# A mixed mLSTM and gMLP encoder on one core: three heads' ways down by Strassen's seven products, and values tile by tile

## The chip, the cores and the metric

One core of a Trainium2 chip runs the whole program. The metric is the device time of one execution in microseconds (us), the median of several runs. The engines are TensorE (PE in the profile; its weight loads are PEld), VectorE (DVE), ScalarE (ACT), GpSimd (POOL) and SyncE (SP), which here only issues DMAs.

## The reference, cut to what matters

The input has 512 tokens of 1024 numbers. Two layers each run a SwiGLU feed-forward network (FFN), a mixer, a second FFN and a gated embedding, each followed by a residual and a layer norm. The mixer of layer 0 is the mLSTM, and the change is in it alone:

```
def mlstm_mixer(x, w_in, b_in, conv_w, norm_g, w_out):
    proj = x @ w_in + b_in                                   # 1024 -> q, k, v, z, gates
    qk, v, z, gates = jnp.split(proj, [...], axis=-1)
    qk = jax.nn.silu(causal_depthwise_conv(qk, conv_w))      # 4 taps
...
    h = mlstm_cell(q, k, v, ig, fg)                          # 4 heads, q and k 256 wide, v 512 wide
    h = ((h - mu) * lax.rsqrt(var + LN_EPS)).reshape(B, S, ML_INNER) * norm_g
    h = (h * jax.nn.sigmoid(z)).astype(x.dtype)
    return h @ w_out                                         # 2048 -> 1024: the way down
```

A head's way down is a product of its 512 x 512 piece of h (tokens by features) with its 512 x 1024 piece of w_out, and the four heads' products are added up.

## The kernel before, in words

**Precision.** Every large product is made from two halves of each operand: a high half (whi, xh, hh) rounded to fp32r and a low half (wlo, xl, hl) with the rest. `mm3` issues three matmuls for one: high by high, low by high, high by low (lines 263 to 265). A matmul of 128 rows by 512 columns is the unit that this document counts.

**Weights.** The class `Weights` holds one list of weight tiles for the whole program, in the order in which TensorE takes them. SyncE loads a raw tile (wraw; three buffers); `fill` splits it into a free pair of whi and wlo, four of which are in the pool "main" and two in "extra" during the mLSTM. ACT makes whi (L188). VectorE makes wlo by a subtraction (L194), or, where the caller says `low="dma"`, ACT writes the negated low half and GpSimd's queue adds the raw tile to it by an accumulating DMA (L191, L192). `take` hands the next pair to the code that issues matmuls; `release` frees it and splits the next tile in the list, so the split's instructions stand in the engines' queues at the place of the release.

**mLSTM, one head after another** (`mlstm`, heads h = 0 to 3):

- `project_qk` makes four tiles, q0, q1, k0, k1, each of 24 matmuls (tile qps). VectorE then does the convolution (pad, one acc and three more, L933 to L938), ACT the silu, and ACT and VectorE the split (qh, ql, L268 and L269).
- `project_v` makes v token block by token block: for each of four blocks 24 matmuls over the four quarters of the weights (vps), then VectorE adds the bias (vf, L969), and a split follows (vh, vl).
- `scores` makes S for the four blocks j (sps, 24 matmuls); ACT makes the decay (ex), VectorE multiplies (sf, L1010) and a split follows (sh, sl). The banks alternate between the two sets of four PSUM banks, "up" and "dn".
- `project_z` makes z0 and z1 (zps, 24 matmuls each); ACT takes the sigmoid (sz) and VectorE multiplies by the norm's gain (L981).
- `mix` makes h for t = 3, 2, 1, 0 (nps, 60 matmuls in all). VectorE and, for one small power, GpSimd normalise each t in a chain of some eleven instructions (L1037 to L1049, ending in hn).
- z2 and z3 follow; then the way down of the head before (`down`, tile dps, 96 matmuls): for each token block four tiles of weights by two halves of the columns, and VectorE adds the two banks to the residual xt (L565, L563).
- `gate_turn` transposes hn (hps, 16 small matmuls, L1064), VectorE multiplies by sz (hzf, L1067), and a split gives hh and hl. In the last head the four transposes stand between the token blocks of the way down of head 2, and the last head's own way down with the norm follows.

**Strassen in the FFNs.** The class `Group` makes a product of 512 tokens, 512 features and 1024 columns from seven half-size products instead of eight. A product is twelve matmuls (gps). `Weights.forms` lists the seven weight tiles for it: b11, b21, t2 = (b22 − b12) + b11, t1, b12, b22, b21, of which t2 and t1 are each made by two VectorE instructions in place on the raw tiles (L104 and L105, L109 and L110). `form` makes the left operand of a product (fhi, flo; for some of them sums of half size first, L725 to L730), `product` issues the matmuls, `add` adds the two banks to the residual. Products 0, 1 and 3 start a pair of banks; product 2 accumulates on top of product 0, 4, 5 and 6 on top of what is there. The mLSTM doesn't use it before.

Of the kernel before, what the change touches and what calls it, by code (L numbers as in the profile page):

```python
# [16 lines left out]
P = 128  # L17
# [29 lines left out]
class Weights:  # L47
# [4 lines left out]
    def __init__(self, nc, raw_pool, split_pool):  # L52
        self.nc = nc
        self.pools, self.free = {"main": split_pool}, {"main": W_BUFS, "none": 0}
        self.raw_pools, self.raw_bufs = {"raw": raw_pool}, {"raw": RAW_BUFS}
        self.loads, self.left, self.raws = [], [], {}
        self.queues, self.held_raws = defaultdict(deque), defaultdict(deque)
        self.order, self.next_split = [], 0
# [32 lines left out]
    def forms(self, quarter, kind, raw_kind):  # L91

        vec = self.nc.vector
        b11, b12, b22, b21 = (self.add_load(quarter(i, j), n, raw_kind)
                              for i, j, n in ((0, 0, 2), (0, 1, 1), (1, 1, 1), (1, 0, 2)))
        raw = self.raws

        def as_loaded(j):  # L100
            return lambda: (raw[j], (j,))

        def t2():
            vec.tensor_sub(raw[b12], raw[b22], raw[b12])  # L104
            vec.tensor_add(raw[b11], raw[b12], raw[b11])  # L105
            return raw[b11], ()

        def t1():
            vec.tensor_sub(raw[b21], raw[b21], raw[b11])  # L109
            vec.tensor_sub(raw[b11], raw[b22], raw[b11])  # L110
            return raw[b11], (b11,)

        return [(kind, (b11,), as_loaded(b11)), (kind, (b12, b22, b21), as_loaded(b21)), (kind, (), t2),
                (kind, (), t1), (kind, (), as_loaded(b12)), (kind, (), as_loaded(b22)), (kind, (), as_loaded(b21))]
# [22 lines left out]
    def load(self, only=None, between=None):  # L137


        for kind, queue in self.queues.items():  # L140
            held = self.held_raws[kind]
            while held and not self.left[held[0]]:
                held.popleft()
            if queue and len(held) < self.raw_bufs.get(kind, 0) and only in (None, kind):
# [4 lines left out]
                size = 2048 if kind == "raw" else 1024  # L149
                name = "wraw" if kind == "raw" else "wquarter"  # L150
                raw = self.raw_pools[kind].tile([P, size], F32, name=name, tag=name)
# [13 lines left out]
    def fill(self, most=1000, low=None):  # L165
        while most and self.next_split < len(self.order):
# [19 lines left out]
            for i in range(parts):  # L186
                s = slice(i * shape[1] // parts, (i + 1) * shape[1] // parts)
                self.nc.scalar.activation(hi[:, s], src[:, s], AF.Copy)  # L188
                if low == "dma":
# [3 lines left out]
                else:  # L193
                    (low or self.nc.vector).tensor_sub(lo[:, s], src[:, s], hi[:, s].bitcast(F32))  # L194
# [38 lines left out]
def hybrid_trunk(ctx: ExitStack, tc, x, p, ln_g, ln_b, ffn1_wgu, ffn1_wd, ffn2_wgu, ffn2_wd,  # L233
# [21 lines left out]
    ps_dn = ctx.enter_context(tc.tile_pool(name="ps_dn", bufs=4, space=PSUM))  # L255
# [18 lines left out]
    def dn_bank(name):  # L274
        return ps_dn.tile([P, 512], F32, name=name, tag="dn")
# [78 lines left out]
    def ml_weights():  # L354
# [3 lines left out]
        def o_w(h):  # L358
            add_rows(wout, 4 * h, 4)

        for h in range(HEADS):
# [6 lines left out]
            if h:  # L368
                o_w(h - 1)
# [1032 lines left out]
```

## Time and profile before

| | |
|---|---|
| median of 3 runs | 2247.41 us (2246.97 to 2248.39) |
| the profiled execution's time, its span | 2248.24 us, 2246.5 us |
| mean granted TensorE clock | 0.999 |
| TensorE busy | 2234.0 us, 99% |
| VectorE busy | 1439.3 us, 64% |
| ACT busy | 886.3 us, 39% |
| matmuls recorded | 10649 |
| first q projection of heads 0, 1, 2, 3 | at 387, 451.7, 552.2 and 652.8 us |
| end of the mLSTM's last way down | at 778 us |

A row of the timeline is start, duration, engine, line, operation, output <- inputs, shape, count; in brackets the idle time before it and what ended that. A row of the grouped view is line, engine, operation, output <- inputs, shape, count | busy us, mean ns | idle before and what ended it. Matmuls overlap, so the time of a run of them is read from start to start.

### The profile page before, as it was taken

Reading aid. Unit: us, or ns where it says so; the run is one execution under the profiler, and the core shown is the slowest. Engines: PE = TensorE matmul, PEld = TensorE weight load, DVE = VectorE, ACT = ScalarE, POOL = GpSimd, SP = SyncE. Lnnn points to the kernel's source line nnn. Section 1 sums busy time; section 2 is a strip of 40 time slices with the busy share of each in tenths; the row PEclk is TensorE's granted clock in tenths of the full one; section 3 lists DMA queues with packets and bytes.
Section 4 is the critical chain, followed back from the end, with each engine's and each line's share of the span. In section 5 each row is a group of like instructions: output and inputs, shape, how many; then the busy total and the mean of one; then the engine's idle time right before and its main releaser. Section 6 shows DMA issues by size and latency. Waiting matters only on the chain.

```text
span 2246.5 us, 26356 instructions
## 1 busy us (share of the span) xinstructions
PE 2234.0 (99%) x10649; PEld 1875.2 (83%) x10649; DVE 1439.3 (64%) x2083; ACT 886.3 (39%) x1241; POOL 103.2 (5%) x136
## 2 busy tenths in 40 slices
PE   9999999999999999999999999999999999999998
PEld 8888888888888888888889888888888888888887
DVE  5566667765555656666687566666756566666677
ACT  3333336454544433333344333335344452333332
POOL 1000000111121000000000000000010100000000
PEclk9999999999999999999999999999999999999999
DMA  7322223376674534331333332222356453432221
GB/s 237 114 94 93 94 85 100 81 177 123 150 152 106 155 113 131 104 103 57 112 122 122 111 95 95 94 85 94 122 141 141 104 167 98 130 113 85 84 85 57
DMA packets 200754, 254.08 MB, mean 113 GB/s; under 512 B 5636, under 2 KB 155268, under 8 KB 200632
## 3 DMA queue, kind: packets, MB, share of 16 engines
q1 hardware_dynamic: 166864, 211.83, 29.1%
q0 software_dynamic: 27152, 25.87, 7.8%
q10 hardware_dynamic: 6616, 14.69, 2.0%
q8 instruction: 84, 1.38, 0.2%
q14 instruction: 38, 0.31, 0.0%
HBM read 224.58 MB, written 2.11 MB: 101 GB/s over the span
## 4 chain that ended last, share of the span: by engine, by line
PE 97%; DMA 1%; ACT 1%; issue 1%; DVE 0%; SPq 0%; POOL 0%; DVEq 0%; POOLq 0%
PE fps L265 13%; PE fps L263 13%; PE fps L264 13%; PE gps L265 6%; PE gps L263 6%; PE gps L264 6%; PE dps L264 5%; PE dps L265 5%; PE dps L263 5%; PE gups L263 1%; PE zps L263 1%; PE gvps L265 1%; PE zps L265 1%; PE gups L264 1%; PE gups L265 1%; PE zps L264 1%
## 5 line engine op out<-in xcount | busy, mean ns | idle before, releaser
L263 PE MATMUL fps<-xh,whi 128*128 128x512 f32 x1312 | 510.7, 389 | 0.0
L264 PE MATMUL fps<-xl,whi 128*128 128x512 f32 x1312 | 510.5, 389 | 0.0
L265 PE MATMUL fps<-xh,wlo 128*128 128x512 f32 x1312 | 510.4, 389 | 0.0
L194 DVE TENSOR_TENSOR wlo<-wraw,whi 128x1024 fp32r<-128x1024 f32 (+1 forms) x284 | 341.7, 1217 | 183.3 <-ACT whi L188 182.2
L188 ACT ACTIVATE whi<-wraw 128x1024 fp32r<-128x1024 f32 (+1 forms) x333 | 344.2, 1048 | 219.3 <-PE fps L264 103.2
L264 PEld LDWEIGHTS fps<-xl,whi 128*128 128x128 f32 x1312 | 246.3, 188 | 51.2
L265 PEld LDWEIGHTS fps<-xh,wlo 128*128 128x128 f32 x1312 | 246.3, 188 | 51.1
L263 PEld LDWEIGHTS fps<-xh,whi 128*128 128x128 f32 x1312 | 246.3, 188 | 50.9
L194 DVE TENSOR_TENSOR wlo<-wquarter,whi 128x1024 fp32r<-128x1024 f32 x112 | 137.2, 1225 | 202.1 <-ACT whi L188 202.1
L188 ACT ACTIVATE whi<-wquarter 128x1024 fp32r<-128x1024 f32 x112 | 118.7, 1060 | 237.8 <-PE gps L265 177.8
L265 PE MATMUL gps<-whi,flo 128*128 128x512 f32 x448 | 174.3, 389 | 0.0
L264 PE MATMUL gps<-wlo,fhi 128*128 128x512 f32 x448 | 174.3, 389 | 0.0
L263 PE MATMUL gps<-whi,fhi 128*128 128x512 f32 x448 | 174.3, 389 | 0.0
L790 ACT ACTIVATE sg<-fps 128x512 f32<-128x512 f32 x80 | 47.9, 598 | 280.8 <-PE fps L265 280.8
L565 DVE TENSOR_TENSOR xt<-xt,gps 128x512 f32<-128x512 f32 x224 | 143.0, 679 | 0.0
L268 ACT ACTIVATE fhi<-h 128x512 fp32r<-128x512 f32 x112 | 69.4, 625 | 115.9 <-DVE h L726 45.8
L263 PE MATMUL dps<-whi,hh 128*128 128x512 f32 x256 | 101.5, 396 | 0.0
L264 PE MATMUL dps<-wlo,hh 128*128 128x512 f32 x256 | 100.5, 393 | 0.0
L265 PE MATMUL dps<-whi,hl 128*128 128x512 f32 x256 | 100.3, 392 | 0.0
L269 DVE TENSOR_TENSOR flo<-h,fhi 128x512 fp32r<-128x512 f32 x112 | 75.6, 687 | 36.4 <-ACT fhi L268 36.4
L264 PEld LDWEIGHTS gps<-wlo,fhi 128*128 128x128 f32 x448 | 84.1, 188 | 17.5
L263 PEld LDWEIGHTS gps<-whi,fhi 128*128 128x128 f32 x448 | 84.1, 188 | 17.4
(277 smaller groups left out, 3852.4 us busy)
## 6 DMA issues: line engine op xcount, KB each, us to landing
wraw<-in_ffn_wgu_dram SPq DMA_DIRECT2D x79, 1024.0 KB, 5.4
wquarter<-in_ffn_wd_dram SPq DMA_DIRECT2D x64, 512.0 KB, 3.8
wlo<-wraw POOLq DMA_DIRECT2D x49, 512.0 KB, 7.6
wraw<-in_ml_w_in_dram SPq DMA_DIRECT2D x24, 1024.0 KB, 5.7
wraw<-in_gm_w_in_dram SPq DMA_DIRECT2D x15, 1024.0 KB, 5.6
wraw<-in_ffn_wd_dram SPq DMA_DIRECT2D x12, 1024.0 KB, 5.0
wraw<-in_ffn_wgu_dram SPq DMA_DIRECT2D x17, 512.0 KB, 3.9
wraw<-in_ml_w_out_dram SPq DMA_DIRECT2D x8, 1024.0 KB, 5.3
```

Source lines behind the costliest of these rows:

```text
L188: self.nc.scalar.activation(hi[:, s], src[:, s], AF.Copy)
L194: (low or self.nc.vector).tensor_sub(lo[:, s], src[:, s], hi[:, s].bitcast(F32))
L263: mm(ps, st[0], mv[0], start=start, stop=False, skip_group_check=more)
L264: mm(ps, st[0], mv[1], start=False, stop=False, skip_group_check=more)
L265: mm(ps, st[1], mv[0], start=False, stop=stop, skip_group_check=more)
L268: sca.activation(hi, src, AF.Copy)
L269: vec.tensor_sub(lo, src, hi.bitcast(F32))
L565: vec.tensor_add(dst, dst, ps)
L790: sca.activation(sg, ps, AF.Silu)
```

## The change

**The ways down of heads 0, 1 and 2 go by `Group`**, and their products are spread over the head that follows. A function `step` does, in this order: add the product before to the residual, issue the next product, release its weight pair (which splits the next tile of the list), and make the form for the product after the next. Heads 1 to 3 call it after q1 (product 0), k0 (product 1), k1 (product 2), after v's quarters 0, 1 and 3 (products 3, 4, 5), and after z3 (product 6; in the last head between the second and third transposes). The addition of product 5 stands after the scores, that of product 6 right behind product 6. `ML_SLOTS` puts the seven weight forms at these places in the list of weights. They come from two raw loads per head: one sits in one of the three raw buffers for three uses, the other in the tile that holds the norm's two vectors (now one tile, "gb", loaded just before the last way down). Raw buffers are therefore freed out of order (`raw_free`). Forms made in place never get their low half by DMA.

**v of heads 1 to 3** goes over weight quarters outside and token blocks inside: four up banks are open at once, so the four vf, vh and vl all come in the last quarter. Head 0 stays as it was.

**Around them:** all scores of heads 1 to 3 use the up banks; z2 moves into the mixing, between t = 1 and t = 0; t = 1 of the mixing and the transposes of odd t use dn banks, which are handed out by number, and those that hold a group's sums are pinned; hf of heads 0 to 2 is kept whole, without a split after the transposes; fewer weight tiles are released with `low="dma"` (16 in place of 34). The last head's own way down stays a plain one of 96 matmuls.

```diff
-    def forms(self, quarter, kind, raw_kind):
+    def forms(self, kind, b11, b12, b22, b21):
...
-                if low == "dma":
+                if low == "dma" and make not in self.in_place:
...
+    ML_SLOTS = (1, 2, 3, 4, 5, 7, 11)
...
             if h:
-                o_w(h - 1)
-        o_w(HEADS - 1)
+                tiles = W.order[at:]
+                del W.order[at:]
+                k = 4 * h - 4
+                j0, j1 = W.add_load(kp(wout)[:, k:k + 2, :], 3), W.add_load(kp(wout)[:, k + 2:k + 4, :], 3, "gb")
+                left, right = ((slice(None), slice(None), slice(c, c + 512)) for c in (0, 512))
+                down_w = W.forms("", (j0, left), (j0, right), (j1, right), (j1, left))
+                for i, tile_i in enumerate(tiles):
+                    W.order.append(tile_i)
+                    if i in ML_SLOTS:
+                        W.order.append(down_w[ML_SLOTS.index(i)])
+        add_rows(wout, 4 * HEADS - 4, 4)
...
         def add(self):
+
             r = self.next_add
+            if r == self.next_product:
+                return
             self.next_add += 1
             i, j = self.TO[r]
             for e, ps in enumerate(self.banks[r % 2]):
-                residual(2 * i + e, j, ps, False)
+                residual(2 * i + e, j, ps, r in self.first)
+                if r >= 5:
+                    del pinned[id(ps)]
...
                     W.release(low="dma")
+                    if i:
+                        step()
...
+                banks = [up_bank("vps") for _ in range(TB)]
+                for k in range(4):
+                    w = W.take()
+                    for t, ps in enumerate(banks):
+                        for kb in (2 * k, 2 * k + 1):
+                            mm3(ps, xs(kb, t * P, (t + 1) * P), [a[:, kb % 2] for a in w], kb == 0, kb == KB - 1)
+                        if k == 3:
+                            take(t, ps)
+                    W.release(low="dma" if k < 2 else None)
+                    if k != 2:
+                        step()
                 return vh, vl
...
-                W.release(later=i < 2, low="dma")
-                run_affine()
+                W.release(later=h == 0 or i > 0)
+                if h == 0:
+                    run_affine()
...
-                    ps = (dn_bank if j % 2 else up_bank)("sps")
+                    ps = (dn_bank if j % 2 and h == 0 else up_bank)("sps")
...
-                    bank = up_bank if t >= 2 else dn_bank
+                    if t == 0:
+                        between()
+                    bank = dn_bank if t == 1 else up_bank
...
+            def step(later=False):
+
+                if group is not None:
+                    group.add()
+                    group.product()
+                    W.release(later=later)
+                    group.form()
...
-                hn = mix(h, ss, v)
-                W.refill(4)
-                for i in range(2, 4):
-                    project_z(h, sz, i)
...
-                if prev is not None:
-                    down(prev, h == 1, low=[None, None, "dma", "dma"] if last else ["dma"] * 4,
-                         between=turn if last else None)
-                else:
-                    norm = Norm(0, 1)
-                if not last:
+                hn = mix(h, ss, v, lambda: project_z(h, sz, 2))
...
+                project_z(h, sz, 3)
+                if h < HEADS - 1:
+                    step(True)
+                    if group is not None:
+                        group.add()
                     hs, turn = gate_turn(h, hn, sz)
                     for t in range(TB):
                         turn(t)
-                prev = hs
-            down(prev, False, norm)
+                    group = Group(hs, fpool, h == 0)
+                    group.form()
+                    group.form()
+                    W.refill(4)
+            hs, turn = gate_turn(h, hn, sz)
+            for t in range(TB):
+                turn(t)
+                if t == 1:
+                    step(True)
+                    group.add()
+            W.refill(4)
+            norm = Norm(0, 1)
+            down(hs, False, norm)
```

The changed kernel's line numbers are higher than those of the profile before, by 13 in `mm3` and `split` and by up to 65 in the mLSTM. Three places in the order of VectorE's instructions follow, each before and after the change.

**VectorE while head 1's q and k are projected.** acc and pad belong to the convolution, ql is the low half of q or k. Before:

```order
L938 SCALAR_TENSOR_TENSOR acc<-pad,cols,acc 128x512 x3
L269 TENSOR_TENSOR ql<-acc,qh 128x512
L933 MEMSET pad 128x3
L936 TENSOR_SCALAR acc<-pad,cols 128x512
L938 SCALAR_TENSOR_TENSOR acc<-pad,cols,acc 128x512 x3
L269 TENSOR_TENSOR ql<-acc,qh 128x512
```

After, the same stretch from q1's convolution to the first addition of the group (wraw<-wraw are the two weight sums of t1, hf<-hf the sums of the left operand, flo its low half, xt<-xt,gps the addition of product 0):

```order
L282 TENSOR_TENSOR ql<-acc,qh 128x512
L110 TENSOR_TENSOR wraw<-wraw 128x2x512
L111 TENSOR_TENSOR wraw<-wraw 128x2x512
L207 TENSOR_TENSOR wlo<-wraw,whi 128x1024
L756 TENSOR_TENSOR hf<-hf 128x2x256
L757 TENSOR_TENSOR hf<-hf 128x2x256
L282 TENSOR_TENSOR flo<-hf,fhi 128x512
L972 MEMSET pad 128x3
L975 TENSOR_SCALAR acc<-pad,cols 128x512
L977 SCALAR_TENSOR_TENSOR acc<-pad,cols,acc 128x512 x3
L282 TENSOR_TENSOR ql<-acc,qh 128x512
L594 SCALAR_TENSOR_TENSOR xt<-xt,gps 128x512 x2
```

Six instructions of the group have come between two convolutions that stood next to each other, and the addition stands behind the second.

**VectorE from the values to the scores of head 1.** vf, vl belong to v, sf and sl to the scores. Before:

```order
L269 TENSOR_TENSOR vl<-vf,vh 128x256 x2
L969 TENSOR_TENSOR vf<-vps,vb 128x512
L269 TENSOR_TENSOR vl<-vf,vh 128x256 x2
L194 TENSOR_TENSOR wlo<-wraw,whi 128x1024
L1010 SCALAR_TENSOR_TENSOR sf<-sps,ex 128x512
```

After:

```order
L1009 TENSOR_TENSOR vf<-vps,vb 128x512
L282 TENSOR_TENSOR vl<-vf,vh 128x256 x2
L207 TENSOR_TENSOR wlo<-wraw,whi 128x1024
L596 TENSOR_TENSOR xt<-xt,gps 128x512 x2
L207 TENSOR_TENSOR wlo<-wraw,whi 128x1024
L1070 SCALAR_TENSOR_TENSOR sf<-sps,ex 128x512
```

An addition (of product 4) and a second low half stand ahead of the first sf. The four rounds of vf and vl in front of these rows are as many as before; they were one per 24 matmuls of vps, and now all four belong to the last 24.

**VectorE at the end of the last head.** hzf and hl follow the transposes, dps is a plain way down. Before:

```order
L1067 TENSOR_TENSOR hzf<-hps,sz 128x512
L269 TENSOR_TENSOR hl<-hzf,hh 128x4x128
L194 TENSOR_TENSOR wlo<-wraw,whi 128x1024 x2
L565 TENSOR_TENSOR xt<-xt,dps 128x512 x2
L1067 TENSOR_TENSOR hzf<-hps,sz 128x512
L269 TENSOR_TENSOR hl<-hzf,hh 128x4x128
L565 TENSOR_TENSOR xt<-xt,dps 128x512
```

After, from the end of the normalising on:

```order
L207 TENSOR_TENSOR wlo<-wraw,whi 128x1024 x3
L1040 TENSOR_SCALAR sz<-sz,cols 128x512
L1132 TENSOR_TENSOR hzf<-hps,sz 128x512
L282 TENSOR_TENSOR hl<-hzf,hh 128x4x128
L1132 TENSOR_TENSOR hzf<-hps,sz 128x512
L282 TENSOR_TENSOR hl<-hzf,hh 128x4x128
L596 TENSOR_TENSOR xt<-xt,gps 128x512 x2
```

The transposes' work, which was spread between the blocks of the way down of head 2, now stands close together behind three low halves, and the addition of product 6 behind its first half.

165 lines of the change are left out of this document (98 added, 67 removed).

## The prediction

> **What bounds the kernel now.** First the page, its busy times and its chain of waits:
>
> ```profile
> PE 2234.0 (99%) x10649; PEld 1875.2 (83%) x10649; DVE 1439.3 (64%) x2083; ACT 886.3 (39%) x1241; POOL 103.2 (5%) x136
> PE 97%; DMA 1%; ACT 1%; issue 1%; DVE 0%; SPq 0%; POOL 0%; DVEq 0%; POOLq 0%
> ```
>
> TensorE is busy for 99% of the span and is 97% of the chain that ended last. A matmul taken away there is time taken away, as long as nothing makes TensorE wait. Second, the windows view of one head of the mLSTM, all engines (each cell is busy us and a count; then granted clock, DMA share, GB/s):
>
> ```profile
> 450.00:551.00 101.00, 101.00 (x489) 85.00 (x488) 57.63 (x120) 48.40 (x71) 14.60 (x17) 1.00 0.62 149
> ```
>
> In these 101 us TensorE has no gap at all, at full clock, and VectorE (third cell) works for 57%. A mean hides where VectorE's work is bunched, and the change puts its new work on VectorE at fixed places. So the question is whether VectorE's answers still come before TensorE asks for them.
>
> **Part 1, what goes: 36 matmuls in each of three heads.** The windows view of tile dps on TensorE for the ways down after heads 1, 2 and 3, then TensorE's timeline at the first one's two ends, and at one Strassen product in a feed-forward stage:
>
> ```profile
> 527.00:552.00 25.00, 22.56 (x96) 1.00 0.79 172
> 627.00:653.00 26.00, 22.57 (x96) 1.00 0.78 168
> 729.00:753.80 24.80, 23.31 (x96) 1.00 0.48 126
> ```
>
> ```profile
> 528.17 0.40 PE L263 MATMUL dps<-whi,hh 128*128 128x512 f32 x1
> ...
> 550.57 0.38 PE L1064 MATMUL hps<-ident,hn 128*128 128x128 f32 x2
> ...
> 862.75 0.39 PE L263 MATMUL gps<-whi,fhi 128*128 128x512 f32 x1
> ...
> 865.47 0.39 PE L263 MATMUL fps<-xh,whi 128*128 128x512 f32 x1
> ```
>
> The first way down takes 550.57 − 528.17 = 22.40 us. The second has the same busy time and gets the same 22.40. The third is broken up by transposes and 0.75 busier; part of that is records overlapping at the breaks, so I take 22.7 (22.4 to 23.15). Together 67.5. A product of twelve matmuls takes 2.72, and 21 of them 57.1. That saves 10.4. If the products ran at the pace of the ways down, 22.40/96 = 0.233 each, they would cost 58.8 and save 8.7.
>
> Fewer weight tiles get their low half by a DMA, which removes a wait that the grouped view shows today:
>
> ```profile
> L264 PE MATMUL vps<-wlo,xh 128*128 128x512 f32 x128 | 49.9, 390 | 0.2 <-DMA wlo<-wraw 0.2
> L264 PEld LDWEIGHTS vps<-wlo,xh 128*128 128x128 f32 x128 | 24.0, 188 | 5.5 <-DMA wlo<-wraw 0.7
> ```
>
> [...]
>
> **Part 2, what comes: VectorE's chain before product 2.** Product 2 accumulates into the banks that product 0 used, so it waits for VectorE to have added product 0 to the residual. That addition stands behind the convolutions of q and k, two pairs of weight sums, the splits and a pair of half sums. VectorE takes all that in order; nothing can overtake. Its timeline in head 0 (the convolution), then in a feed-forward stage (the Strassen work), and the page's row for the high half of a weight tile:
>
> ```profile
> 462.39 0.49 DVE L936 TENSOR_SCALAR acc<-pad,cols 128x512 f32<-128x512 f32 x1 [0.25 <-ACT pad L934]
> ...
> 465.19 0.06 DVE L933 MEMSET pad<- 128x3 f32 x1
> ...
> 469.47 0.68 DVE L269 TENSOR_TENSOR ql<-acc,qh 128x512 fp32r<-128x512 f32 x1
> ...
> 862.47 1.22 DVE L109 TENSOR_TENSOR wquarter<-wquarter 128x1024 f32<-128x1024 f32 x1
> 863.72 1.22 DVE L110 TENSOR_TENSOR wquarter<-wquarter 128x1024 f32<-128x1024 f32 x1
> ...
> 866.81 1.22 DVE L194 TENSOR_TENSOR wlo<-wquarter,whi 128x1024 fp32r<-128x1024 f32 x1 [1.86 <-ACT whi L188]
> 867.95 1.22 DVE L194 TENSOR_TENSOR wlo<-wraw,whi 128x1024 fp32r<-128x1024 f32 x1
> 869.09 0.69 DVE L725 TENSOR_TENSOR h<-h 128x512 f32<-128x512 f32 x1
> ...
> 871.26 0.69 DVE L269 TENSOR_TENSOR flo<-h,fhi 128x512 fp32r<-128x512 f32 x1 [0.76 <-ACT fhi L268]
> 871.87 1.27 DVE L565 TENSOR_TENSOR xt<-xt,gps 128x512 f32<-128x512 f32 x2
> ```
>
> ```profile
> L188 ACT ACTIVATE whi<-wraw 128x1024 fp32r<-128x1024 f32 (+1 forms) x333 | 344.2, 1048 | 219.3 <-PE fps L264 103.2
> ```
>
> A convolution is 2.8 (462.39 to 465.19), a pair of weight sums 2.5, the wait for a high half 1.05 where ACT can only start when VectorE has made its input, a low half 1.15 (866.81 to 867.95), the half sums with the wait for fhi 2.2 (869.09 to 871.26), a split's low part 0.6, the first of two additions 0.65. From the end of q's first projection: 0.9 until the copy is there for the convolution (0.2 to see TensorE's end, 0.7 for a 128x512 copy, an estimate from the rows' 0.69), then 2.8 + (2.5 + 1.05 + 1.15) + 2.8 + 0.6 + (2.5 + 1.05 + 1.15) + 2.2 + 0.6 + 2.8 + 0.6 + 0.65 = 23.35 us. TensorE gets there after three projections of 24 matmuls (5.44 each, twice a product) and two products: 16.3 + 5.4 = 21.8. So it waits 1.6 in heads 2 and 3.
>
> In head 1 VectorE comes late to the start as well, since head 0 ends in a burst on it. TensorE's rows of one mixing and one set of transposes, then VectorE's at the end of head 0 and of head 1's mixing:
>
> ```profile
> 450.04 0.38 PE L1064 MATMUL hps<-ident,hn 128*128 128x128 f32 x2
> 451.70 0.49 PE L263 MATMUL qps<-xh,whi 128*128 128x512 f32 x1
> ...
> 510.07 0.28 PE L1027 MATMUL nps<-vh,sh 128*128 128x258 f32 x1
> ...
> 517.27 0.39 PE L263 MATMUL zps<-xh,whi 128*128 128x512 f32 x1
> ```
>
> ```profile
> 448.55 4.62 DVE L194 TENSOR_TENSOR wlo<-wraw,whi 128x1024 fp32r<-128x1024 f32 x4
> 453.09 0.87 DVE L981 TENSOR_SCALAR sz<-sz,cols 128x512 f32<-128x512 f32 x2
> 454.07 0.69 DVE L1067 TENSOR_TENSOR hzf<-hps,sz 128x512 f32<-128x512 f32 x1
> ...
> 456.07 0.68 DVE L1067 TENSOR_TENSOR hzf<-hps,sz 128x512 f32<-128x512 f32 x1
> ...
> 526.95 1.22 DVE L194 TENSOR_TENSOR wlo<-wraw,whi 128x1024 fp32r<-128x1024 f32 x1
> ```
>
> Measured from the start of a mixing, VectorE ends its normalising at 526.95 − 510.07 = 16.9, plus 0.4 for the sz of the z tile that now stands inside: 17.3. Then four low halves 4.54, sz 0.45, four products with the transposes 2.5, two form splits 1.3 and two more low halves 2.3: 28.4. TensorE has q's first projection done at 7.2 + 5.44 + 5.44 + 1.67 + 5.44 = 25.2, and the convolution could start at 26.1. VectorE is 2.3 late, so product 2 waits 3.9 there. Sum of part 2: 3.9 + 1.6 + 1.6 = **7.1**. Products 3 to 6 have a projection more between them or less VectorE work, and I count no wait.
>
> **Part 3, what comes: z's first tile waits for the scores.** All scores of heads 1 to 3 now lie in the four up banks, so z0 needs the first of them back: VectorE's sf of j = 0 has to have read it. Ahead of that sf now stand four rounds of vf, vh, vl at the end of the last v quarter; before, one round was left. TensorE's rows around the scores, then VectorE's from the last round to sf:
>
> ```profile
> 495.37 0.39 PE L263 MATMUL sps<-qh 128*128 128x512 f32 x1
> ...
> 499.12 0.45 PE L263 MATMUL zps<-xh,whi 128*128 128x512 f32 x1
> ```
>
> ```profile
> 495.57 0.69 DVE L969 TENSOR_TENSOR vf<-vps,vb 128x512 f32<-128x512 f32 x1 [3.50 <-PE vps L265]
> ...
> 498.00 1.23 DVE L194 TENSOR_TENSOR wlo<-wraw,whi 128x1024 fp32r<-128x1024 f32 x1 [0.50 <-ACT whi L188]
> ...
> 500.60 0.69 DVE L1010 SCALAR_TENSOR_TENSOR sf<-sps,ex 128x512 f32<-128x512 f32 x1 [1.37 <-ACT ex L1008]
> ```
>
> A round takes 498.00 − 495.57 − 0.50 = 1.93, and from the last vf to sf are 5.03. From the start of the last v quarter VectorE is held by a weight tile released just then (0.2 + 1.05 + 1.15 = 2.4); the last vf starts at 2.4 + 3 × 1.93 = 8.2, sf at 13.2, and one more high half on ACT ahead of ex makes 14.15; sf is through at 14.85. TensorE is there after 5.44 + 2.72 + (499.12 − 495.37) = 11.9. It waits 2.9 in each of three heads: **8.7**. If the weight tile comes first but ACT fits its high half into a pause, it is 1.0 less per head.
>
> **Part 4, two small ones.** In heads 1 and 2 the second and fourth transposes use the banks of product 6, whose addition stands at 17.3 + 2.3 + 0.45 = 20.05 on VectorE and 7.2 + 10.9 + 2.72 + 0.2 = 21.0 by TensorE: the first half is done at 21.65 while the first transposes end at 21.2. That is 0.5 each, **1.0**. In the last head the addition of product 6 stands behind two rounds of hzf, hh, hl: 17.3 + 3.4 (three low halves) + 0.5 + 2 × 2.0 + 0.65 = 25.85, while TensorE is at 18.1 + 1.67 + 2.72 = 22.5 and wants those banks for the last way down. It waits **3.4**.
>
> The work that I cost at nothing, with its cover: the forms' weight loads are the bytes that were loaded before; the norm's two vectors are loaded just before the last way down and used after it; the z tile that moves inside the mixing gives VectorE's normalising 5.4 us more cover for t = 1.
>
> **Sum**: −10.4 + 7.1 + 8.7 + 1.0 + 3.4 = **+9.8 us**. The profiled execution took 2248.24 and stands 0.8 above the median of 2247.41; on the median that gives **2257.2**.
>
> **Rivals.** *The cover holds* (faster): in the feed-forward stages the same products, 8.16 us apart, show no wait on TensorE, and VectorE is idle 43% of a head. If the chain of part 2 comes out under 21.8 and that of part 3 under 11.9, because ACT and VectorE overlap more than rows laid end to end, all waits go: 2247.4 − 10.4 = 2237. Against it: part 3 is short by 2.9 of 14.85, and no single row there is that wrong. *Only part 2 is covered* (no change): it is the closest, 1.6 of 23.35, but the rest stays: −10.4 + 8.7 + 1.0 + 3.4 = +2.7, 2250. *The products are not cheaper* by as much: 8.7 in place of 10.4 adds 1.7, inside the forecast's range. *The clock falls* (slower still): at the end of the program the windows show what a pause does,
>
> ```profile
> 2236.00:2240.00 4.00, 1.11 (x10) 0.90 (x8) 2.72 (x7) 0.42 (x1) 0.00 (x0) 1.00 0.00 0
> 2240.00:2246.00 6.00, 0.00 (x0) 0.00 (x0) 3.13 (x7) 0.00 (x0) 0.92 (x1) 0.67 0.23 87
> ```
>
> TensorE ends at about 2237.1 and the granted clock is 1.00 up to 2240 and 0.67 over the next 6 us. If it fell to half there, it did so two thirds before the end, near 2242, 4.9 us after the last matmul (an estimate). My longest waits are 3.9 and 3.4, below that. If the clock did fall for one or two products after them, that would add 2.7 to 5.4 each: 2262 or more. [...]
>
> **Chances.** About 0.2%, 4.5 us, is what a measurement here can tell from no change. Cover holds: 0.13. Only part 2 covered: 0.20, within 0.2%. The waits as worked out: 0.60, its own range 2252 to 2263 (gain 8.7 to 10.9, each wait a microsecond either way). The clock falls or loads come late: 0.07. So faster 0.13, same 0.20, slower 0.67. The range reaches from 2244, between the first two rivals, to 2265; it leaves out the first rival and the upper end of the last.
>
> **What would show it.** In the changed kernel's grouped view, tile zps should have idle time released by VectorE's sf, near 8.7 in all; gps by the addition of xt, near 7; dps by the same addition, near 3.4 at the start of the last way down. 252 matmuls of gps in the mLSTM should take 57. I am wrong if TensorE shows no idle time between about 450 and 760, or if its waits there are ended by weight tiles or DMAs.

## The result, and the profile after

The changed kernel takes 2273.07 us (median of 4 runs, 2271.45 to 2275.38) against 2247.78 beside it: 1.0115 times the time before, 95% interval 1.0103 to 1.0127. It is 25.3 us slower. The prediction had 9.8 us slower, and the time lies above its range. The mean granted clock of its runs is 0.992 to 0.994, where the profile before had 0.999.

The changed kernel's page has TensorE and VectorE busier, and one head takes longer than the 101 us of before. The page's busy times, then the windows view of heads 1 and 2 (all engines, then granted clock, DMA share, GB/s):

```profile
PE 2238.5 (99%) x10613; PEld 1875.8 (83%) x10613; DVE 1505.3 (66%) x2161; ACT 884.3 (39%) x1241; POOL 84.1 (4%) x118
```

```profile
450.90:558.70 107.80, 101.48 (x475) 84.58 (x473) 78.77 (x146) 48.13 (x71) 8.97 (x12) 0.97 0.41 113
558.70:664.50 105.80, 101.44 (x475) 84.55 (x473) 75.68 (x142) 48.26 (x71) 9.02 (x12) 0.97 0.40 105
```

TensorE issues 36 matmuls fewer (10613 for 10649: 84 for 96 in each of three heads) and is yet busy for 4.5 us longer. In head 1 it is idle for 6.3 us of 107.8, and the granted clock is 0.97 where it was 1.00. The waits of TensorE (line waited for: us in total, times, longest):

```profile
PE zps L276 <- DVE sf L1070: 7.6, 3, 2.5
PE dps L276 <- DVE xt L596: 5.5, 3, 3.2
PE gps L276 <- DVE xt L594: 3.8, 1, 3.8
PE gps L276 <- DVE xt L596: 3.7, 2, 1.8
```

These are the places of the prediction: z0 behind sf in three heads, product 2 behind the addition of product 0 (3.8 in head 1, 1.8 in heads 2 and 3), the last way down behind the addition of product 6 (3.2). Two waits of dps of 1.13 were not in the forecast; they lie at the ends of the two layers' second FFNs. VectorE's rows before product 2 of head 1 and before z0 show what TensorE waits for:

```profile
480.92 0.68 DVE L282 TENSOR_TENSOR ql<-acc,qh 128x512 fp32r<-128x512 f32 x1
481.52 1.28 DVE L594 SCALAR_TENSOR_TENSOR xt<-xt,gps 128x512 f32<-128x512 f32 x2
...
517.88 0.76 DVE L282 TENSOR_TENSOR vl<-vf,vh 128x256 fp32r<-128x256 f32 x2 [0.49 <-ACT vh L281]
519.14 1.22 DVE L207 TENSOR_TENSOR wlo<-wraw,whi 128x1024 fp32r<-128x1024 f32 x1 [0.49 <-ACT whi L201]
520.28 1.28 DVE L596 TENSOR_TENSOR xt<-xt,gps 128x512 f32<-128x512 f32 x2
521.48 1.22 DVE L207 TENSOR_TENSOR wlo<-wraw,whi 128x1024 fp32r<-128x1024 f32 x1
522.68 0.69 DVE L1070 SCALAR_TENSOR_TENSOR sf<-sps,ex 128x512 f32<-128x512 f32 x1
```

VectorE works almost without a gap right up to both answers. (ACT's exponentials, which sf needs too, end at 522.65, at the same time as VectorE's last low half.) What the forecast's sum did not have stands right behind the pauses. TensorE's timeline at product 2 of head 1, and the windows view before, in, and after it:

```profile
482.34 0.47 PE L276 MATMUL gps<-whi,fhi 128*128 128x512 f32 x1 [3.80 <-DVE xt L594]
482.65 0.39 PE L277 MATMUL gps<-wlo,fhi 128*128 128x512 f32 x1
...
483.37 0.63 PE L277 MATMUL gps<-wlo,fhi 128*128 128x512 f32 x1
483.80 0.63 PE L278 MATMUL gps<-whi,flo 128*128 128x512 f32 x1
...
486.36 0.56 PE L278 MATMUL gps<-whi,flo 128*128 128x512 f32 x1
486.76 0.39 PE L276 MATMUL vps<-whi,xh 128*128 128x512 f32 x1
```

```profile
480.00:482.30 2.30, 0.00 (x0) 0.00 (x0) 2.27 (x5) 2.30 (x4) 0.85 (x1) 1.00 0.00 0
482.30:486.80 4.50, 4.46 (x13) 3.57 (x14) 4.29 (x8) 3.74 (x6) 0.43 (x1) 0.62 0.61 117
486.80:490.00 3.20, 3.20 (x16) 2.61 (x15) 3.20 (x5) 1.06 (x1) 0.40 (x1) 1.00 0.87 212
```

The first matmuls after the pause run at the old pace, 0.23 us apart. About a microsecond later they are 0.43 apart ("half pace" below; a "slow stretch" is a time at half clock), and some 3.4 us after that at full pace again: the granted clock is 0.62 over this window. The product takes 4.42 (482.34 to 486.76) in place of 2.79. The same stands behind all seven long pauses of the mLSTM: the three products 2, the three z0, and the last way down. So what the forecast lacked is the clock, and it fell here after pauses of 1.8 us and more.

**Where 24 us went**, from start to start in the two profiled executions (2272.41 and 2248.24, 24.2 apart; a pause costs about 0.15 more than the idle time that the wait shows: 3.95 for 3.80 at product 2 of head 1): pauses at product 2 7.9, at z0 8.1, at the last way down 3.4, at the ends of two FFNs 2.6, together 22.0. Slow stretches: 3 × 1.62 at product 2, 3 × 1.69 in the z0 and z1 pair, 1.4 at the last way down, together 11.3. Products in place of ways down −8.8, the DMA wait −0.5. The sum is +24.0.

### The profile page after: what moved, and what is told of

Its sections match the earlier page's. It is cut to its first block, busy times and chain, and to the rows that moved or that the text cites. A ratio compares the mean times of both kernels' runs of the same rounds, so it can differ in the third digit from the quotient of the medians.

```text
span 2270.7 us, 26333 instructions
## 1 busy us (share of the span) xinstructions
PE 2238.5 (99%) x10613; PEld 1875.8 (83%) x10613; DVE 1505.3 (66%) x2161; ACT 884.3 (39%) x1241; POOL 84.1 (4%) x118
## 4 chain that ended last, share of the span: by engine, by line
PE 74%; DVE 5%; ACT 1%; issue 0%; POOL 0%; DVEq 0%; ACTq 0%; POOLq 0%
PE fps L278 10%; PE fps L276 10%; PE fps L277 10%; PE gps L276 5%; PE gps L278 5%; PE gps L277 5%; PE dps L276 3%; PE dps L277 3%; PE dps L278 3%; PE gups L276 1%; PE gups L277 1%; PE gvps L276 1%; PE gups L278 1%; PE gvps L278 1%; PE gvps L277 1%; DVE wlo L207 1%
## 5 line engine op out<-in xcount | busy, mean ns | idle before, releaser
L207 DVE TENSOR_TENSOR wlo<-wraw,whi 128x1024 fp32r<-128x1024 f32 (+1 forms) x311 | 375.0, 1219 | 210.4 <-ACT whi L201 209.3
L276 PE MATMUL gps<-whi,fhi 128*128 128x512 f32 x532 | 209.4, 394 | 7.5 <-DVE xt L594 3.8
L277 PE MATMUL gps<-wlo,fhi 128*128 128x512 f32 x532 | 209.5, 394 | 0.0
L278 PE MATMUL gps<-whi,flo 128*128 128x512 f32 x532 | 209.3, 394 | 0.0
L596 DVE TENSOR_TENSOR xt<-xt,gps 128x512 f32<-128x512 f32 x258 | 165.0, 681 | 0.5 <-PE gps L278 0.5
L276 PEld LDWEIGHTS gps<-whi,fhi 128*128 128x128 f32 x532 | 100.7, 189 | 29.9 <-ACT whi L201 8.6
L278 PEld LDWEIGHTS gps<-whi,flo 128*128 128x128 f32 x532 | 101.2, 190 | 21.6
L277 PEld LDWEIGHTS gps<-wlo,fhi 128*128 128x128 f32 x532 | 100.8, 189 | 21.4
L469 ACT ACTIVATE xf<-xps,cols 128x128 f32<-128x128 f32 x160 | 59.9, 454 | 56.7 <-PE xps L464 56.5
L566 POOL TENSOR_TENSOR rs<-rs,eps_pow 128x1 f32<-128x1 f32 x32 | 20.6, 644 | 1584.8 <-DVE rs L565 1584.8
```

Source lines behind the costliest of these rows:

```text
L207: self.nc.vector.tensor_sub(lo[:, s], src[:, s], hi[:, s].bitcast(F32))
L276: mm(ps, st[0], mv[0], start=start, stop=False, skip_group_check=more)
L277: mm(ps, st[0], mv[1], start=False, stop=False, skip_group_check=more)
L278: mm(ps, st[1], mv[0], start=False, stop=stop, skip_group_check=more)
L469: sca.activation(xf[:, k], ps[:, k], AF.Identity, scale=col("ln_g", norm.at + 4 * g + k), bias=col("ln_b", norm.at + 4 * g + k))
L566: pool.tensor_tensor(rs[:, 1:2], rs[:, 0:1], eps_pow, op=OP.pow)
```

## The experiments

### The addition of product 0 moved ahead of the convolution

In `project_qk`, for i = 2 and 3, the addition that `step` would make comes before the copy to pad and the convolution (`early` is the group's `add`):

```diff
                     ps = banks.popleft() if banks else project()
+                    if i >= 2:
+                        early()
                     ch = (i // 2 * QK + h * DQK) // P + i % 2
```

> The changed kernel, in which VectorE adds products 0 and 1 to the residual ahead of the convolutions of k0 and k1 and no longer behind them. Theory 1 (each pause of TensorE costs its own length, and if it fills about half or more of one 3.4 us window of a fixed grid, TensorE runs the next window at half clock, 1.6 us more): the addition comes 3.4 us earlier, product 2's waits of 3.95, 1.99 and 2.00 fall to about 0.5, 0 and 0, and the three slow products (4.41 in place of 2.79) go too: -7.4 - 4.9 = -12.3 against 2273.07, about 2261. Theory 2 (the slow matmuls are slow because VectorE, ACT and the DMAs are busy at that moment, not because of the pause): the waits go, the 4.41 stays: -7.4, about 2266. Theory 3 (the chain on VectorE is as long wherever the addition stands): no change, 2273.

It took 2260.94 (2257.87 to 2262.32), 1.006 times the time before (1.0045 to 1.0075), 12.1 less than the changed kernel. Product 2's waits are down to 0.6 in all, in two pieces of 0.3:

```profile
PE gps L276 <- DVE xt L594: 0.6, 2, 0.3
```

In heads 2 and 3 product 2 follows without a pause, and its matmuls are 0.23 apart, although VectorE, ACT and the DMAs do the same work beside it. Theory 1 stands; theories 2 and 3 fall.

### Banks handed out in the order in which they were given back

```diff
                 if r >= 5:
-                    del pinned[id(ps)]
+                    at = pinned.pop(id(ps))
+                    dn_order.remove(at)
+                    dn_order.append(at)
```

> The changed kernel, in which a dn bank that a group gives back goes to the end of the queue of banks, so that the next user gets the bank that was given back first (product 5's, not product 6's). Theory (the waits of dps on the addition of xt come from the banks being handed out by the order in which they were taken): the two waits of 1.29 at the ends of the second FFNs go, -2.6; the last way down of the mLSTM then waits only for the first hl, at 23.2 us from the start of the mixing where TensorE is at 22.5, so 0.7 in place of 3.5, -2.8, and its slow stretch goes, -1.4: about -6.8, 2266. Rival (those waits are due to VectorE's queue whichever bank is used): no change, 2273.

It took 2267.26 (2263.57 to 2267.28), 1.0086 (1.0071 to 1.0101), 5.8 less. All three waits of dps are gone, so the order of the banks was their cause. A pause that the expectation lacked took the place of one of them, in the norm of the last way down, where VectorE is busy with the splits of the next FFN:

```profile
PE xps L464 <- DVE xt L573: 1.8, 1, 1.8
```

### Product 6 between the scores and z0

`ML_SLOTS` ends in 7, 7 in place of 7, 11; `step()` and the addition of product 6 stand after the scores, and no longer after z3 or between the transposes.

> The changed kernel, in which product 6 stands between the scores and z0 in heads 1 to 3 and no longer after z3. Theory (z0 waits until VectorE's first sf, 2.5 us after TensorE is there, whatever TensorE does meanwhile): product 6 takes 2.79 in that time, so the wait of 2.7 and the slow stretch of 1.7 go in three heads, -13.2; in the last head no product stands between the transposes any more, and the way down waits for the first hl behind four low halves, at about 24.3 from the start of the mixing where TensorE is at 19.8: 4.5 in place of 3.5 and again a slow stretch, +1.0: about 2261. Rival (the weight split and the two additions that come along hold up sf by as much as product 6 takes): the wait stays and the time is 2273 or more.

It took 2260.78 (2260.33 to 2261.67), 1.0062 (1.0046 to 1.0079), 12.3 less. z0 waits no more. In the last head the way down now waits for hh:

```profile
PE dps L276 <- ACT hh L281: 3.8, 1, 3.8
```

This run also holds a plain sight of the clock. Product 2 of heads 2 and 3 comes after equal pauses, and only one is slow. TensorE's timeline and the windows view of the two:

```profile
583.83 0.47 PE L276 MATMUL gps<-whi,fhi 128*128 128x512 f32 x1 [1.83 <-DVE xt L595]
...
588.20 0.45 PE L276 MATMUL vps<-whi,xh 128*128 128x512 f32 x1
...
685.67 0.47 PE L276 MATMUL gps<-whi,fhi 128*128 128x512 f32 x1 [1.84 <-DVE xt L595]
...
688.54 0.39 PE L276 MATMUL vps<-whi,xh 128*128 128x512 f32 x1
```

```profile
583.80:588.20 4.40, 4.37 (x13) 3.46 (x14) 4.22 (x7) 3.73 (x6) 0.34 (x1) 0.62 0.63 119
685.70:688.50 2.80, 2.80 (x12) 2.30 (x13) 2.66 (x5) 2.77 (x6) 0.00 (x0) 1.00 0.98 186
```

The work is the same, the pause is the same, and one product takes 4.37 and the other 2.87. So neither the neighbours' work nor the pause's length alone decided here. By the clock in the trace the slow stretch begins at 584.88. If the clock goes by windows of 3.4133 us (the slow stretches of the changed kernel begin whole multiples of that apart, as those of the next run do), others begin at 581.47 and, 30 windows later, at 683.87. The first pause (582.00 to 583.83) then lies wholly within a window; the second (683.84 to 685.67) begins 0.03 us ahead of one, which leaves 1.81 in it. So this pair lies at the very bound.

### Pauses of many lengths, measured by themselves

The kernel before, with this ahead of every product of the FFNs:

```diff
+            def pause(src):
+                d = fpool.tile([P, 64], F32, name="pd", tag="pd", bufs=1)
+                vec.tensor_copy(d, src[:, :64])
+                for _ in range(probe[0] * 7 % 24):
+                    vec.tensor_scalar(d, d, 1.0, None, op0=OP.mult)
+                probe[0] += 1
+                nc.tensor.transpose(up_bank("probe")[:64, :P], d, ident)
```

> The kernel before the change, with a pause of TensorE put ahead of each of the 112 Strassen products of the four FFNs: a chain of 0 to 23 small VectorE instructions reads the last bank and TensorE transposes its result into a spare bank. The transposes' results are not used, so nothing of the computation is left out. Grid theory (a window of 3.41 us of a fixed grid that is idle for about half or more, between 40% and 54% by the three waits seen, makes the next window run at half clock): no pause under 1.3 us is followed by slow matmuls, of those of 1.7 to 2.0 about half are, of those over 3.4 all; the slow stretches last about 3.4 us and end on multiples of 3.41. Rival 1 (a timer from the last matmul, of about 1.8 us): all pauses over 1.8 are followed by slow matmuls. Rival 2 (only a window that is idle throughout counts): none under 3.4 is.

One run, 2748.61 us with all its pauses. In the timeline, from the first FFN on, 113 pauses are longer than 0.3 us. Counted by their length, with how many were followed by matmuls at half pace (of those of 1.5 to 2.0 us it is one in nine, fewer than expected):

| pause, us | followed by half pace | not |
|---|---|---|
| 0.3 to 1.5 | 0 | 26 |
| 1.5 to 2.0 | 1 | 8 |
| 2.0 to 2.5 | 4 | 7 |
| 2.5 to 3.0 | 7 | 2 |
| 3.0 to 3.5 | 6 | 3 |
| over 3.5 | 49 | 0 |

Two pauses of equal length with different ends, in the windows view (the pause, then what follows):

```profile
103.70:106.30 2.60, 0.00 (x0) 0.00 (x0) 2.19 (x10) 0.14 (x1) 0.00 (x0) 1.00 0.91 284
106.40:110.00 3.60, 3.60 (x17) 2.97 (x18) 1.69 (x3) 0.54 (x1) 0.00 (x0) 1.00 0.24 81
1220.00:1222.60 2.60, 0.00 (x0) 0.00 (x0) 2.26 (x13) 1.54 (x2) 0.00 (x0) 1.00 0.00 0
1222.70:1224.20 1.50, 1.50 (x7) 1.28 (x8) 1.50 (x3) 0.00 (x0) 0.00 (x0) 0.94 0.00 0
1224.30:1227.30 3.00, 3.00 (x9) 2.31 (x8) 0.55 (x1) 0.20 (x1) 0.00 (x0) 0.50 0.38 100
1227.30:1230.00 2.70, 2.70 (x13) 2.24 (x12) 1.81 (x2) 1.38 (x2) 0.00 (x0) 0.98 0.80 277
```

The first pause, of 2.67, costs itself. After the second, of 2.70, TensorE goes on at full clock for 1.3 us and then at half clock for 3.4, from 1224.0 to 1227.4 (worked out from the clock's shares 0.94, 0.50 and 0.98 in the last three rows). By the clock that the trace has, there are 67 slow stretches, spread over 2500 us; 45 last 3.41 us and 22 last 6.83, and all end at times that leave the same remainder when divided by 3.4133 us, 2.04 to 2.06. On this grid a window's end splits the first of the two pauses into 0.8 and 1.9 us; of the second, 2.1 lie in the window that ends at 1224.0. If one cuts the run into these windows and asks how much of one window was idle, a bound of 1.9 to 2.0 us sorts 112 of the 113 pauses: up to 1.83 none was followed by half clock, from 1.99 on all were, and of the four between (1.92 to 1.94) one. In the kernels with the change the bound lay a little lower: windows idle for 1.82 to 1.84 were followed by half clock in all seven cases, and the one with 1.81 was not. So in these runs half clock followed where some 53% (1.82 us) to 58% (1.99 us) of a window or more was idle. Of the 26 pauses under 1.5 us none was followed by half pace, of the 38 of 1.5 to 3.5 us 18 were, by how much of them fell into one window, and of the longer ones all 49. Both rivals fall: the one without a grid by the pauses of 2.67 and 2.70, the one that wants an idle window throughout by the 18 pauses under 3.4 that were followed by half pace.

The stretches of 6.83, two windows, have a lower bound of their own. A window at half clock that was itself idle for 0.79 us or more was followed by another (22 of 22), one idle for 0.75 or less was not (0 of 67; in the run with the addition moved one of 0.66 was). So here a pause that reached 0.79 us or more into its slow window cost a second one.

### The low half of v left out

In heads 1 to 3 `take` makes vh by two copies and no vl; GpSimd sets vl to zero.

```diff
+                    if h:
+                        sca.activation(vh[:, t, :HV], vf[:, :HV], AF.Copy)
+                        sca.activation(vh[:, t, HV + 2:], vf[:, HV:], AF.Copy)
+                        return
                     split(vh[:, t, :HV], vl[:, t, :HV], vf[:, :HV])
...
+                if h:
+                    pool.memset(vl.bitcast(F32), 0.0)
```

> The changed kernel, which leaves out the low half of v in heads 1 to 3 (vl is set to zero once per head by GpSimd), so that a round at the end of v is one VectorE instruction and not three with a wait for ACT between them. Theory (z0 waits because four rounds of 1.9 stand ahead of the first sf): the four rounds shrink by more than the wait of 2.5, so z0's waits (7.6) and their slow windows (5.1) go: about 2260. Rival (z0's wait is set by ACT's exponentials or by the low halves of weights, not by the rounds): z0 still waits about 2.5.

One run, 2263.61. z0's three waits fall from 7.6 to 2.3 us, and no slow stretch follows them:

```profile
PE zps L276 <- DVE sf L1076: 2.3, 3, 0.8
```

The rounds carry most of the wait, 1.8 of 2.5 us. For most of the rest the timeline of this run shows the rival's ACT: VectorE is free 0.55 before the first sf and waits for the exponentials (ex), in all three heads alike:

```profile
522.15 0.69 DVE L1076 SCALAR_TENSOR_TENSOR sf<-sps,ex 128x512 f32<-128x512 f32 x1 [0.55 <-ACT ex L1074]
```

The run is 3.6 slower than the 2260 expected. The 2.3 of waits are a part of it; product 2 of head 1, with two slow windows in this one execution, took 5.26 in place of 4.41.

### All three edits, and another place for the left operands

The first run joins the three edits; in the last head the refill of weight pairs after z2 is dropped, and one pair at a time is refilled after the first and second transposes:

```diff
-                W.refill(4 if h == 0 else 2)
+                if h < HEADS - 1:
+                    W.refill(4 if h == 0 else 2)
...
                 turn(t)
+                if t < 2:
+                    W.refill()
```

> The three edits of the runs before together, and in the last head VectorE makes the first product of hzf, hh, hl ahead of the low halves of the last way down's weights, no longer behind four of them. Theory (the change saves 8.9 for cheaper products and 0.5 for a DMA wait, and everything it lost were pauses and the slow windows behind them): what is left are about 0.6 at product 2 of head 1, 1.4 around product 6, 1.1 at the last way down, 1.8 at the norm after it and 0.7 at the changes between kinds of matmul, none of them long enough for the clock to fall: 2247 - 9.4 + 5.6 = about 2243, faster than before. Rival (VectorE's work per head is too much for the gaps that TensorE leaves, so the waits come back at other places): 2247 or more.

The second run differs in one line only:

```diff
-        with stage_pool("extra", EXTRA) as extra, stage_pool("ml_parts") as near, stage_pool("forms", 2) as fpool, \
+        with stage_pool("extra", EXTRA) as extra, stage_pool("forms", 2) as fpool, stage_pool("ml_parts") as near, \
```

> As the run beside it, with the pool of the left operands fhi and flo laid into memory ahead of the pool that holds vh (whose rows of 514 numbers make the tiles behind it start 32 bytes off a multiple of 64). Theory (products in the mLSTM take 0.2328 us a matmul and not 0.2267 as in the FFNs because of where fhi lies): the 21 products take 2.72 and not 2.79, 1.5 less than the run beside it. Rival (something else sets the pace): the same time and 2.79.

No run shows the 0.7 for changes between kinds of matmul in the first sum: in the changed kernel's mLSTM the step from q or v to a product is 0.235 us and back 0.233 (medians), against 0.227 within q and v.

They took 2247.75 (1.0004, 0.9995 to 1.0013) and 2248.02 (1.0002, 0.9993 to 1.0011), the time before and not 2243. Head 1 became 1.2 us shorter than before the change and head 2 2.3, but from the last head's start to the next FFN it is 3.8 longer. The waits of the first of the two runs:

```profile
PE dps L276 <- DVE xt L595: 2.4, 2, 2.1
PE xps L463 <- DVE xt L572: 1.8, 1, 1.8
...
PE dps L276 <- ACT hh L281: 1.0, 1, 1.0
```

The rival was right for the last head. There VectorE's transposed products, the weight splits and the norm stand close together; before, the way down of head 2 lay between them. In the second run, with the left operands in another place, the products have another pace. TensorE's first product of head 1, in the changed kernel and then in this run:

```profile
461.90 0.39 PE L276 MATMUL gps<-whi,fhi 128*128 128x512 f32 x1
...
464.70 0.39 PE L276 MATMUL qps<-xh,whi 128*128 128x512 f32 x1
```

```profile
461.71 0.39 PE L276 MATMUL gps<-whi,fhi 128*128 128x512 f32 x1
...
464.44 0.39 PE L276 MATMUL qps<-xh,whi 128*128 128x512 f32 x1
```

2.80 becomes 2.73 for the same twelve matmuls. Yet the median gains nothing. By the traces the clock took it: in the last way down both runs have a pause of 2.1 us. In the first run's trace it is cut by the end of a window, no window is idle for more than 1.6, and the clock stays full; in the second's nearly all of it falls into one window, idle for 2.2 in all, and two windows at half clock follow. From the last head's transposes to the next FFN the second run is 2.0 longer. The windows view of that place, the first run and then the second:

```profile
762.00:769.00 7.00, 4.88 (x23) 3.56 (x24) 6.09 (x13) 2.24 (x6) 0.55 (x1) 1.00 0.62 204
762.20:769.00 6.80, 5.47 (x18) 4.09 (x17) 5.47 (x12) 2.14 (x5) 1.10 (x2) 0.50 0.60 216
```

The times of all eleven executions of each bear this out as far as their mean clock tells. Of the first kernel's, eight took 2247.4 to 2248.2 and three, with the lowest clock (0.997), 2249.4 to 2250.0; of the second's, three took 2245.9 to 2246.7 (0.998) and eight (0.997) 2247.9 to 2249.1. At like clock the second is 1.3 to 1.6 faster by the medians, as expected; by this reading it met the slow windows more often. Why more often is open.

### The last head on its own terms

Product 6 ahead of z0 in heads 1 and 2 only; in the last head it stays between the transposes, and two kinds of splits are held back. The added `W.refill(2)` stands in the last head, after the scores; `after0` is called after the sums of the last way down's second block:

```diff
-                    W.release(low="dma" if k < 2 else None)
+                    hold = h == HEADS - 1 and k == 3
+                    W.release(later=hold, low="dma" if k < 2 else None)
                     if k != 2:
-                        step()
+                        step(hold)
...
                 else:
                     group.add()
+                    W.refill(2)
...
-            W.refill(4)
             norm = Norm(0, 1)
-            down(hs, False, norm)
+            down(hs, False, norm, after0=lambda: W.refill(4))
```

> The early addition and the order of banks as before, product 6 ahead of z0 in heads 1 and 2 alone; in the last head product 6 stays between the transposes, the two splits after the values are held back until the scores are through (so that they don't stand ahead of sf), and the splits for the next FFN are held back until the second block of the last way down. Theory (run e5 saved 1.2 in head 1 and 2.3 in head 2 and lost 3.8 from the last head on, where VectorE's transposes, splits and norm are bunched): heads 1 and 2 keep their 3.5, the last head saves 3.0 on products and loses 1.0 at z0 and about 0.5 elsewhere, with no pause long enough for the clock: 5 under the kernel before, about 2242. Rival (VectorE's work in the last head is too much in any order): as e5, 2247 to 2248.

It took 2241.99 (2241.66 to 2242.35), 0.9977 (0.9968 to 0.9986) of the time before. It is the first of these kernels that is faster, by 0.23%. TensorE's waits in it:

```profile
PE zps L276 <- DVE sf L1077: 0.6, 1, 0.6
PE gps L276 <- DVE xt L594: 0.5, 2, 0.3
PE gps L276 <- DVE xt L596: 0.4, 2, 0.2
```

No pause is longer than 0.7 us in the mLSTM, and no slow stretch is left. With the left operands moved as well:

> Run e8 with the pool of fhi and flo laid ahead of the pool that holds vh, as in run e6. Theory (the products' pace of 0.2328 comes from where fhi lies): the 21 products take 2.72 in place of 2.79, 1.5 less than e8's 2242.0, about 2240.5. Rival (the pace changes but VectorE then is what TensorE waits for, as e6 came out no faster than e5): 2242.

2241.0 (2240.78 to 2241.35), 0.9973 (0.9963 to 0.9984): another 1.0 of the expected 1.5. Products after a short wait still take 2.80 to 2.85, and the others 2.72.

## Why the prediction was wrong

- **The saving.** Forecast 10.4, measured 8.8 and 0.5. The rows of the FFN gave a price (2.72) that the products did not have in the mLSTM (2.79). It was a rival of the prediction, with 8.7 as its number, and that came true. In the run with the left operands first, with another order of the pools in memory, the same product took 2.73 where it took 2.80. That the rows of 514 numbers do it is not shown, since several tiles moved along. (The heading of the prediction's part 1 has 36 matmuls for each head; it is 12, and 36 in all. Its sum went by 96 and 84.)
- **Product 2.** Forecast 3.9 + 1.6 + 1.6 = 7.1, measured 3.95 + 1.99 + 2.0 = 7.9. The chain held to 0.4 a head (one of its rows, the wait for a high half, was 1.19 and not 1.05, twice), and moving the addition all but removed the wait.
- **z0.** Forecast 8.7, measured 8.1. The rounds were 1.85 each, not 1.93. The run without vl shows that they are most of it, and product 6 covers it.
- **Transposes in heads 1 and 2.** Forecast 1.0, measured nothing. The estimate was 0.45 between two ends of about 21 us.
- **The last way down.** Forecast 3.4, measured 3.4.
- **Banks in the FFNs.** Not in the prediction. The change hands out dn banks by a queue of its own everywhere, so the FFNs' ways down got the bank of product 6 and not that of product 5, and waited 1.3 twice. The changed kernel shows it in `dn_bank`, which every stage calls; the prediction weighed it for the mLSTM alone.
- **The clock: the step that failed.** The prediction read the end of the program, where the granted clock is 1.00 for some 3 us after the last matmul and 0.67 over the next 6, as a delay of 4.9 us, and set the longest pauses (3.9 and 3.4) against that. It gave the case 0.07, counted two places at 2.7 to 5.4 each, and put nothing into its sum. But a single end of a program told neither the bound nor the place of the windows: in the later runs a pause counted by how much of one window of 3.41 us it filled, from 1.8 to 2.0 us on. The trace of before has the fall, to 0.50, at 2242.05. Counted back from it in such windows, the 4.9 was the last 1.5 us of one, too little to count in those runs, and one whole idle window of 3.4. In the changed kernel's profile all seven pauses of 1.8 us and more were followed by a slow stretch, of 1.4 to 1.7 each, 11.3 us in all. With this term and the 2.6 of the banks the rest of the forecast's sum, 9.8, becomes 23.7; measured were 24.2 in the profiled executions. That the terms which the forecast did have come to 10.1 is luck in part: their errors, of −1.0 to +1.1, cancel.

So three of the four waits stood where the forecast put them, within 0.8 us each. What failed is their price: each long one had a second part, the slow window after it, that the sum set at nothing.

## What to carry to other kernels

Where TensorE was otherwise never idle, a wait of 1.8 us or more on it cost up to nearly twice in the changed kernel: itself, and 1.4 to 1.7 us of half clock after it, seven times of seven. Several waits of half a microsecond were cheaper than one of two: in the run on the last head, with none over 0.7 us in the mLSTM, no slow stretch is left. So products that can be moved are best put where TensorE would wait. When work is taken from TensorE, look for what VectorE did in its shadow: here more than half of the saving of 9 us came out (5.1 us, 6.0 with the left operands moved), and only after the order of VectorE's work had been set anew for the last head, where that shadow had been longest.

## What the runs showed of the hardware

- The granted clock of TensorE fell to 0.50 for stretches of 3.41 us or twice that. In the changed kernel's trace the seven of the mLSTM last 3.41 us each and begin at 483.30 us and 12, 31, 43, 62, 74 and 85 times 3.4133 us later; in the run with pauses 67, spread over 2500 us, end on one such grid. There, cut into windows by it, a window that was idle for 1.9 to 2.0 us or more was followed by one at half clock (with a bound of 1.95, 112 of 113 pauses); in the kernels with the change those idle for 1.82 to 1.84 were (seven of seven). From half clock it took less: a slow window idle for 0.79 us or more was followed by another (22 of 22). The grid did not start with the program: the slow stretches end, divided by 3.4133 us, at a remainder of 0.4, 1.2, 2.0 and 2.4 us in four traces (of the changed kernel and the first three edits).
- Kernels with pauses of 1.8 us and more varied more from run to run: two by some 4 us (2257.87 to 2262.32, 2263.57 to 2267.28), a third by 1.3 (2260.33 to 2261.67), the first one without pauses over 0.7 us by 0.7. In the first two the fastest run also has the highest mean clock (0.997 and 0.995); that the place of the grid makes the difference fits, but was not shown run by run.
- The same twelve matmuls of head 1's first product took 2.80 us in the changed kernel and 2.73 in the run with another order in memory of the pools around their left operand.
